# A hybrid decoder trunk on one core: the matrix engine's order written by hand, with a clock that counts product steps

## The chip, the core and the metric

The kernel runs on one core of a Trainium2 chip. A core has a matrix engine (TensorE; PE in the profile, and PEld for its weight loads), a vector engine (VectorE, DVE), a scalar engine (ScalarE, ACT), GpSimd (POOL), and SyncE (SP), whose queue issues every DMA of this kernel. Each engine works off its own queue in the order in which the program put it there. Engines wait for each other through semaphores. The metric is the device time of one execution in microseconds (us).

## What is computed

One decoder layer for 2,048 tokens of width 1,024, in float32. Three groups of heads share one input projection and one output projection. Two of the three kinds (HGRN2, here "h", and GLA, here "g") are gated linear recurrences; retention ("r") is one with a fixed decay. Cut to what matters:

```python
h = rms_norm(x) * (1.0 + sc1) + sh1
proj = h @ w_in[l]                               # 1024 -> all heads' q, k, v, gates
o_r = retention_chunkwise(rotary(rq), rotary(rk) * 64**-0.5, rv, log_gamma)
o_h = gated_state_chunkwise(silu(hq), key_h, hi, log_f)      # S_t = diag(f_t) S_{t-1} + k_t^T v_t
o_a = gated_state_chunkwise(aq, ak * 32**-0.5, av, g_log)    # o_t = q_t S_t
o = concat([rms_norm(o_r)*silu(rg), rms_norm(o_h)*silu(hg), rms_norm(o_a)*silu(ag)]) * head_gain
x = x + g1 * (o @ w_out)
h = rms_norm(x) * (1.0 + sc2) + sh2
u = conv3(h @ w_up) + conv_b                     # causal, depthwise
x = x + g2 * ((silu(gate(u)) * val(u)) @ w_down)
out = rms_norm(x) * final_gain
```

The six vectors sh1 to g2 come from `c` through the matrix w_ada (48 rows of 128 outputs).

## The kernel before

**Products.** Float32 accuracy comes from splitting each operand in a rounded high part (hi) and the rest (lo), and from three fast matmuls hi·hi, hi·lo, lo·hi (`split3`, L180 to L182). So each weight piece (128x1024, 512 KB) is loaded, cast to hi on ACT, and subtracted to lo on DVE (`piece`, L166 and L167; `tf512`, L224 and L225; with a gain for the output projection, L172 and L175). The 38 pieces of a block (30 of w_in, 8 of w_out) are prepared anew for each of the four blocks.

**Mixer.** The 2,048 tokens are four blocks of 512. In each block seven units run in the order h0, g, h1, h2, h3, r0, r1. A unit projects (`cf_gemm`, `tf_gemm`, `tf512`), and then has a chain: seven levels for h and g (`gated`), each of which multiplies q by k on PE in float32 (`lv`, L397), copies the result under a mask into `at` on DVE (L406, ACT for the last two), and multiplies q and k by decays on DVE (L411, L413), on which the next level's matmuls wait; then a transpose of k (`kT`), the state update (`u`), the output (`o`), a norm (`post`), and a transpose (`oT`) for the output projection `out_half`, whose results are called y. An r unit has a rotation on DVE (L573 to L579), transposes (`qT`, `kT`), scores (`scr`, L600), `u`, `o`, `post`. The chain of a unit is written behind the projections of the next unit (`flush`), in a block of priority `CHAIN`; Tile's scheduler decides how the two mix on each engine. The second norm (`ss`, `bc`) writes h2 and x1 to DRAM.

**Conditioning.** The 16 rows of w_ada that the first norm needs are reduced at the start (`ada`: 12 on DVE at L148, 4 on POOL and ACT), the other 32 rows in four groups of eight behind the first four units of block 0.

**Channel mixer.** After `mix.close()` new pools are opened. Stage `up` runs twice (s = 0 for tokens of blocks 0 and 1, s = 1 for 2 and 3), 22 columns f each, with 7 products of 12 matmuls for each f (X, Y, Z in PSUM; Strassen-like sums, so 28 operands B are made from h2 before, and 7 operands A for each f); a convolution on DVE and ACT follows, and `gd` goes to DRAM. Stage `down` then runs over four blocks in two halves of 11 steps (d in PSUM), reads `gd` back (`gr`, cast to G), and ends each block with the third norm and the output.

The order of all engines is the scheduler's, by priorities. SP's queue is one list too: a load that stands behind a store waits until the store can go.

Of the kernel before, what the change touches and what calls it, by code (L numbers as in the profile page):

```python
# [16 lines left out]
P = 128  # L17
# [27 lines left out]
POOL_K = (0, 2, 4, 6)  # L45
# [3 lines left out]
CHAIN = 3000  # L49
FIRST = [("hfh0_0", 1), ("hqh0_0", 0), ("vgh0_0_0", 2)]  # L50


@with_exitstack
def trunk(ctx, tc, xT, vecs, cvec, cst, rope, msk, wada, win, walow, wgla, wout, wup, wdown, out):
# [3 lines left out]
    mix = ctx.enter_context(ExitStack())  # L58
    sb = lambda n, b: mix.enter_context(tc.tile_pool(name=n, bufs=b))
    ph = sb("h", 1)  # L60
    pu = sb("unit", 2)
    p1 = sb("const1", 1)
# [4 lines left out]
    pp = mix.enter_context(tc.tile_pool(name="ps", bufs=1, space=PSUM))  # L67
# [7 lines left out]


    def early_ps(name):
        return pp.tile([P, 512], F32, tag="acc", name=name, bufs=4)
# [79 lines left out]
    def piece(src, name, gain=None, ahead=50):  # L158

        with tc.high_priority(offset=ahead):  # L160
            raw = pw.tile([P, 1024], F32, tag="wraw", name="r" + name, bufs=NRAW)
            nc.sync.dma_start(raw[:], src)
            hi = pw.tile([P, 1024], F32R, tag="whi", name="h" + name)
            lo = pw.tile([P, 1024], F32R, tag="wlo", name="l" + name)
            if gain is None:
                S.copy(hi[:], raw[:])  # L166
                V.tensor_tensor(lo[:], raw[:], hi[:], op=ALU.subtract)  # L167
            else:
# [4 lines left out]
                for i, g in enumerate(gain):  # L173
                    sl = slice(i * n, (i + 1) * n)
                    V.scalar_tensor_tensor(lo[:, sl], raw[:, sl], g, hi[:, sl], op0=ALU.mult, op1=ALU.subtract)  # L175
        return hi, lo
# [13 lines left out]
    def cf_gemm(name, src, parts=(slice(0, TB),)):  # L190
        hi, lo = ready.pop(name, None) or piece(src, name)
        ps = acc_ps("ps" + name)
        for ts in parts:
            for k in range(KD):
                sl = slice(k * P, (k + 1) * P)
                split3(ps[:, ts], (hi[:, sl], lo[:, sl]), (h[k][:, 0, ts], h[k][:, 1, ts]), k == 0, k == KD - 1)
        return ps

    def tf_gemm(name, i):
        pss = [acc_ps(f"ps{name}_{j}") for j in range(NCH // 2)]  # L200
        for half in range(2):
            hi, lo = ready.pop(f"{name}_{half}", None) or piece(win[i + half], f"{name}_{half}")
            for c in range(NCH):
                o = pss[c // 2][:, (c % 2) * 256:(c % 2) * 256 + 256]
                for kk in range(4):
# [4 lines left out]
                           k == 0 and c % 2 == 0, k == KD - 1 and c % 2 == 1)  # L210
        return pss

    def tf512(name, i):

        pss = [acc_ps(f"ps{name}_{c}") for c in range(NCH)]
        for q4 in range(4):
            half, sub = q4 // 2, q4 % 2
            src = win[i + half:i + half + 3:2][:, :, sub * 512:(sub + 1) * 512].rearrange("a p n -> p a n")
            with tc.high_priority(offset=50):
# [5 lines left out]
                V.tensor_tensor(lo[:], raw[:], hi[:], op=ALU.subtract)  # L225
            for c in range(NCH):
                cs = slice(c * P, (c + 1) * P)
                for kk in range(2):
# [3 lines left out]
                           (hi[:, :, sl], lo[:, :, sl]), k == 0, k == KD - 1)  # L232
        return pss


    def rstd_bc(acc, name, bc=None, sl=slice(0, TB)):
        c0, n = sl.start // P, (sl.stop - sl.start) // P
        ps = late_ps("ss" + name)
        for c in range(n):
            T.matmul(ps[:, c:c + 1], acc[:, (c0 + c) * P:(c0 + c + 1) * P], ones, start=True, stop=True)  # L240
        return rstd_from(ps, name, bc, sl)

    def rstd_from(ps, name, bc=None, sl=slice(0, TB)):

        n = (sl.stop - sl.start) // P
        x = small("ms" + name, n)
        V.tensor_scalar(x[:], ps[:, 0:n], 1.0 / D, EPS, op0=ALU.mult, op1=ALU.add)
        r = small("rs" + name, n)
        newton(x, r, n)
        ps = late_ps("bc" + name)  # L250
        for c in range(n):
            T.matmul(ps[:, c * P:(c + 1) * P], r[:, c:c + 1].to_broadcast([P, P]), ident, start=True, stop=True)
        if bc is None:
            bc = px.tile([P, TB], F32, tag="bc2", name="rb" + name, bufs=1)
# [751 lines left out]
```

## Time and profile before

| | |
|---|---|
| three runs, median (lowest to highest) | 2848.06 us (2847.24 to 2851.18) |
| the profiled execution's own time | 2853.58 us |
| its span, first to last instruction | 2851.8 us |
| mean granted TensorE clock | 0.962 of full |
| PE busy | 2641.6 us, 93% of the span |
| DVE busy | 2072.0 us, 73% |
| ACT busy | 1141.9 us, 40% |
| DMA moved | 316.94 MB, 111 GB/s over the span |

Durations come from the one profiled execution. "Granted clock" is the share of full speed at which PE was allowed to run in a stretch. A float32 matmul of 128 columns appears as two records, so that "x8" in a row of the timeline stands for four matmuls of the program. In the chain of waits each line is a start, a duration and who held the chain then.

### The profile page before, as it was taken

To read this page: it belongs to the slowest core of one execution; us is meant where nothing else is said; L and a number is where in the kernel's file an instruction comes from. 1 tells how busy PE (TensorE), PEld (TensorE's weight loads), DVE (VectorE), ACT (ScalarE), POOL (GpSimd) and SP (SyncE) were. 2 spreads that over 40 slices of the span, in tenths; PEclk is the share of its full clock that TensorE was granted. 3 is DMA by queue.
4 is the path that set the end of the run, shared out by engine and by line. 5 is a ranking of instruction groups with operands and counts; after the bars stand their busy time and mean duration, and the time that the engine had idled before them with its cause. 6 is when DMAs were issued, how large, how long until landed. Compare 5 with 4: busy or idle time off the path is not lost.

```text
span 2851.8 us, 35540 instructions
## 1 busy us (share of the span) xinstructions
PE 2641.6 (93%) x13396; PEld 2217.7 (78%) x13396; DVE 2072.0 (73%) x3561; ACT 1141.9 (40%) x1869; POOL 116.4 (4%) x189
## 2 busy tenths in 40 slices
PE   5899889998999979998869999989999979999997
PEld 4788777887778868887748888868888868888886
DVE  8887677876778677784678888898888875534442
ACT  4322434334343434332355445555544544332321
POOL 3000000000000000000000000000000000000000
PEclk9989999999999989999979999989999989999998
DMA  6343314131231413212142222232222236645441
GB/s 255 131 138 116 120 59 151 47 130 64 90 111 59 135 49 136 72 60 74 51 171 89 79 79 86 89 133 89 89 83 81 82 132 223 212 148 189 144 141 59
DMA packets 119419, 316.94 MB, mean 111 GB/s; under 512 B 12592, under 2 KB 14160, under 8 KB 119248
## 3 DMA queue, kind: packets, MB, share of 16 engines
q1 hardware_dynamic: 119248, 314.68, 31.4%
q8 instruction: 105, 1.72, 0.2%
q14 instruction: 66, 0.54, 0.1%
HBM read 266.39 MB, written 48.23 MB: 110 GB/s over the span
## 4 chain that ended last, share of the span: by engine, by line
PE 81%; DVE 13%; issue 2%; ACT 2%; DMA 1%; SPq 0%; DVEq 0%; ACTq 0%
PE X L180 6%; PE d L180 6%; PE d L182 6%; PE d L181 6%; PE X L181 6%; PE X L182 6%; PE lvh L397 4%; PE Z L180 3%; PE Z L181 3%; PE Z L182 3%; PE y L180 2%; PE y L181 2%; PE y L182 2%; PE psqkvgr L180 2%; PE psqkvgr L181 2%
## 5 line engine op out<-in xcount | busy, mean ns | idle before, releaser
L180 PE MATMUL X<-B,A 128*128 128x512 f32 x704 | 280.0, 398 | 22.1 <-ACT B L711 16.1
L180 PE MATMUL d<-G,hd 128*128 128x512 f32 x704 | 275.5, 391 | 15.3 <-ACT G L711 15.3
L181 PE MATMUL X<-B,A 128*128 128x512 f32 x704 | 279.3, 397 | 1.0 <-DVE B L712 1.0
L182 PE MATMUL X<-B,A 128*128 128x512 f32 x704 | 278.3, 395 | 0.0
L182 PE MATMUL d<-G,ld 128*128 128x512 f32 x704 | 275.5, 391 | 0.0
L181 PE MATMUL d<-G,hd 128*128 128x512 f32 x704 | 275.4, 391 | 0.0
L886 DVE TENSOR_TENSOR ld<-rd,hd 128x1024 fp32r<-128x1024 f32 x88 | 107.7, 1224 | 152.1 <-ACT hd L885 151.8
L397 PE MATMUL lvh<-qbd,kh 128*128 128x128 f32 x896 | 138.5, 302 | 50.8 <-DVE kh L413 25.5
L397 PEld LDWEIGHTS lvh<-qbd,kh 128*128 128x128 f32 x896 | 122.2, 208 | 72.4 <-issue 27.2
L180 PEld LDWEIGHTS X<-B,A 128*128 128x128 f32 x704 | 134.6, 191 | 55.3 <-ACT B L711 17.5
L180 PEld LDWEIGHTS d<-G,hd 128*128 128x128 f32 x704 | 132.9, 189 | 42.9 <-ACT G L711 15.7
L885 ACT CAST hd<-rd 128x1024 fp32r<-128x1024 f32 x88 | 92.3, 1048 | 182.8 <-PE d L181 176.3
L181 PEld LDWEIGHTS X<-B,A 128*128 128x128 f32 x704 | 135.1, 192 | 30.5 <-DVE B L712 2.9
L182 PEld LDWEIGHTS X<-B,A 128*128 128x128 f32 x704 | 134.9, 192 | 28.2
L181 PEld LDWEIGHTS d<-G,hd 128*128 128x128 f32 x704 | 132.7, 189 | 28.0 <-DVE G L712 0.4
L182 PEld LDWEIGHTS d<-G,ld 128*128 128x128 f32 x704 | 132.8, 189 | 27.5
L180 PE MATMUL Z<-B,A 128*128 128x512 f32 x352 | 138.2, 393 | 9.4 <-ACT B L711 9.4
L182 PE MATMUL psvgh<-hvgh,ha 128*128 128x256 f32 x512 | 146.6, 286 | 0.0
L180 PE MATMUL psvgh<-hvgh,ha 128*128 128x256 f32 x512 | 146.3, 286 | 0.0
L181 PE MATMUL psvgh<-lvgh,ha 128*128 128x256 f32 x512 | 146.1, 285 | 0.0
L181 PE MATMUL Z<-B,A 128*128 128x512 f32 x352 | 138.0, 392 | 3.1 <-DVE B L712 3.1
L182 PE MATMUL Z<-B,A 128*128 128x512 f32 x352 | 137.6, 391 | 0.0
(388 smaller groups left out, 6562.4 us busy)
## 6 DMA issues: line engine op xcount, KB each, us to landing
rd<-wdown SPq DMA_DIRECT2D x88, 512.0 KB, 3.5
wada<-wada SPq DMA_DIRECT2D x48, 512.0 KB, 3.7
rv<-wup SPq DMA_DIRECT2D x44, 512.0 KB, 3.5
rg<-wup SPq DMA_DIRECT2D x44, 512.0 KB, 3.4
gd<-yv SPq DMA_DIRECT2D x44, 512.0 KB, 2.6
gr<-gd SPq DMA_DIRECT2D x88, 256.0 KB, 3.6
x<-xT SPq DMA_DIRECT2D x64, 256.0 KB, 4.8
rvgh<-win SPq DMA_DIRECT2D x32, 512.0 KB, 3.5
```

What stands on the lines that cost most here:

```text
L180: T.matmul(ps, lhs[0], rhs[0], start=first, stop=False, skip_group_check=more)
L181: T.matmul(ps, lhs[0], rhs[1], start=False, stop=False, skip_group_check=more)
L182: T.matmul(ps, lhs[1], rhs[0], start=False, stop=last, skip_group_check=more)
L397: T.matmul(ps[:, c * P:(c + 1) * P].rearrange("p (h n s) -> p h n s", h=2, s=s), kq[:, c * P:(c + 1) * P], rhs, start=True, stop=True)
L885: S.copy(hi[:], raw[:])
L886: V.tensor_tensor(lo[:], raw[:], hi[:], op=ALU.subtract)
```

## The change

1. **PE's order is written by hand.** After unit h0 of block 0, `tc.manual_schedule` keeps PE's instructions in the order of the code. A `Clock` counts: after each product step `adv` adds that step's time (0.227 us a matmul of 512 columns, 0.12 of 256, 0.224 in float32). A chain is now a generator that yields the gap to its next step; when the clock has passed it, the step's matmuls are let in between the projections that are being written. One chain is in its line at a time; the last step (`oT`) follows 12 us later beside the next chain. All other engines are still scheduled; DVE work of a chain has a higher priority.
2. **Weights are kept.** In block 0 each lo part of w_in, and both gained parts of w_out, are stored to DRAM (`keep`); blocks 1 to 3 load them instead of computing them (ACT still casts hi for w_in).
3. **Conditioning rows are spread**: one of the other 32 rows at each weight piece.
4. **Decays ahead**: the products of decays (`decays`) are computed before the chain; in a level the products of q and k come before the masked copy.
5. **One set of pools.** The up and down stages take over the mixer's buffers, ring by ring, and the same PSUM tags; the order is up 0, down 0 and 1, up 1, down 2 and 3. Norms 1, 2 and 3 are cut in two steps (`rstd`) that the clock places between later products. The first norm of block 0 sums its squares on PE.

The core of the diff:

```diff
+M512, M256, MF = 0.227, 0.12, 0.224
+LEVEL_GAP = (3.2, 4.8)
+POST_GAP = 12.0
+class Clock:
+    def at(self, us, fn):
+        heapq.heappush(self.due, (self.t + us, self.n, fn))
+        self.n += 1
+    def _next(self):
+        t, _, fn = heapq.heappop(self.due)
+        self.t = max(self.t, t)
+        fn()
+    def adv(self, us):
+        self.t += us
+        while self.due and self.due[0][0] <= self.t:
+            self._next()
+    def until(self, done):
+        while not done():
+            self._next()
...
+    def keep(key, t):
+        kept[key] = pdr.tile([P, 1024], F32, tag=f"kept{key}", name=f"kept{key}")
+        nc.sync.dma_start(kept[key][:], t.bitcast(F32))
...
-    def piece(src, name, gain=None, ahead=50):
+    def piece(src, name, key, gain=None, ahead=50):
+        if later:
+            ada(later.pop(0), False, True)
...
+            if key + "h" in kept:
+                nc.sync.dma_start(hi[:].bitcast(F32), kept[key + "h"][:])
+                nc.sync.dma_start(lo[:].bitcast(F32), kept[key + "l"][:])
+                return hi, lo
...
             if gain is None:
                 S.copy(hi[:], raw[:])
-                V.tensor_tensor(lo[:], raw[:], hi[:], op=ALU.subtract)
+                if key + "l" in kept:
+                    nc.sync.dma_start(lo[:].bitcast(F32), kept[key + "l"][:])
+                else:
+                    V.tensor_tensor(lo[:], raw[:], hi[:], op=ALU.subtract)
+                    keep(key + "l", lo[:])
...
                 split3(ps[:, ts], (hi[:, sl], lo[:, sl]), (h[k][:, 0, ts], h[k][:, 1, ts]), k == 0, k == KD - 1)
+                adv(3 * M512)
...
         for li, s in enumerate(LEVELS):
...
+            with tc.high_priority(offset=CHAIN):
+                ev = tree[li]
...
+            adv(4 * len(subs) * MF)
+            yield LEVEL_GAP[two]
...
+        yield None
+        for i, o in enumerate(os):
+            yield POST_GAP if i == 0 else 3.0
+            transposed(b, pos + i, o, f"{name}_{i}")
+            adv(4 * MF)
...
+        clock.chain(gated(nm, b, u, pos, kq, decay, subs, qk, selh), 6.0)
+        tok_evac(subs[0][2:], tf_gemm("vg" + nm, 4 * u + 2))
...
+            if b == 0 and i == 0:
+                ctx.enter_context(tc.manual_schedule(engines={mybir.EngineType.PE}))
+                later += range(16, 48)
+            if i == 0 and b:
+                clock.until(lambda: None not in oTs[b - 1])
+                out_finish(b - 1)
+        if b + 1 < NB:
+            norm1_h(b + 1)
+        else:
+            B = low_inputs(0, tmp)
+        clock.until(lambda: None not in oTs[b][:4])
+        out_half(b, 0)
+    clock.until(lambda: None not in oTs[NB - 1])
+    mix.close()
...
+    B, rest = up_inputs(0, B)
+    out_finish(NB - 1, lambda: first.append(up_weights(0, 0)))
+    rest[0]()
+    up_stage(0, first[0], B)
+    clock.until(lambda: ("n2", NB - 1) in done)
+    down_block(0)
+    A, B = down_block(1, lambda: (up_weights(1, 0), up_inputs(1, low_inputs(1, t2k))[0]))
+    up_stage(1, A, B)
+    down_block(2)
+    down_block(3)
```

Three places in the queues show what moves. Names carry block, unit and level: `lvh2_3_8` is level 8 of unit h3 in block 2, `psqkvgr2_1_0` the projection of r1 in block 2, `y3_1_0` the first product of the output projection's second half in block 3.

PE, block 2, where h3's chain meets the r units; before:

```order
L182 MATMUL psqkvgr2_0_3_8183<-hqkvgr2_0_3_8276,ha2_7_5900 128x512
L397 MATMUL lvh2_3_4_8365<-qbd1_108,kh2_3_7776 128x128 x4
L397 MATMUL lvh2_3_8_8374<-qbd1_108,kh2_3_7776 128x128 x4
L584 MATMUL qTr2_0_8330<-c_all_86,rar2_0_8318 128x128 x4
L586 MATMUL kTr2_0_8331<-c_all_86,kkr2_0_8178 128x128 x4
L180 MATMUL psqkvgr2_1_0_8481<-hqkvgr2_1_0_8487,ha2_0_5851 128x512
```

and of the change:

```order
L528 MATMUL lvh2_3_4_8395<-qbh2_3_7778,kh2_3_7661 128x128 x4
L250 MATMUL psqkvgr2_1_0_8258<-hqkvgr2_1_2_8405,ha2_4_5724 128x512
L251 MATMUL psqkvgr2_1_0_8258<-lqkvgr2_1_2_8406,ha2_4_5724 128x512
L252 MATMUL psqkvgr2_1_0_8258<-hqkvgr2_1_2_8405,ha2_4_5724 128x512
L250 MATMUL psqkvgr2_1_0_8258<-hqkvgr2_1_2_8405,ha2_5_5731 128x512
L251 MATMUL psqkvgr2_1_0_8258<-lqkvgr2_1_2_8406,ha2_5_5731 128x512
L252 MATMUL psqkvgr2_1_0_8258<-hqkvgr2_1_2_8405,ha2_5_5731 128x512
L250 MATMUL psqkvgr2_1_1_8259<-hqkvgr2_1_2_8405,ha2_4_5724 128x512
L251 MATMUL psqkvgr2_1_1_8259<-lqkvgr2_1_2_8406,ha2_4_5724 128x512
L252 MATMUL psqkvgr2_1_1_8259<-hqkvgr2_1_2_8405,ha2_4_5724 128x512
L465 MATMUL oTh2_2_0_8418<-c_all_86,oh2_2_0_8299 128x128 x4
```

Before, levels 4 and 8 stand side by side between two projections; in the change nine matmuls of r1's projection and the transpose of h2's output follow level 4, and three more matmuls before level 8 comes; r0's transposes come some 110 rows later, in the output projection.

PE, block 3, around the last transpose `oTr3_1`; before:

```order
L182 MATMUL y3_1_3_11630<-oTr3_0_11491,lwo3_1_1_11604 128x512
L354 MATMUL oTr3_1_11548<-c_all_86,or3_1_11527 128x128 x4
L180 MATMUL y3_1_0_11569<-oTr3_1_11553,hwo3_1_0_11559 128x512
L180 MATMUL y3_1_1_11584<-oTr3_1_11553,hwo3_1_0_11559 128x512
L180 MATMUL y3_1_2_11613<-oTr3_1_11553,hwo3_1_1_11603 128x512
```

and of the change:

```order
L484 MATMUL or3_1_11651<-vr3_1_11022,atr3_1_11641 128x64 x2
L465 MATMUL oTr3_0_11685<-c_all_86,or3_0_11565 128x128 x4
L465 MATMUL oTr3_1_11693<-c_all_86,or3_1_11664 128x128 x4
L250 MATMUL y3_1_0_11813<-oTh3_2_0_11187,hwo3_1_0_11809 128x512
L251 MATMUL y3_1_0_11813<-oTh3_2_0_11187,hwo3_1_0_11809 128x512
```

Before, 36 matmuls of the output projection's second half stand ahead of `oTr3_1`; in the change none does.

SP, at the border from up to down; before (gd1_21 is the last store of stage up):

```order
L814 DMA gd1_21_235<-yv1_21_18575 128x1024
L880 DMA gr0_0_18600<-gd0_0_192 128x512
L880 DMA gr0_1_18605<-gd0_1_193 128x512
L880 DMA gr0_2_18640<-gd0_2_194 128x512
L880 DMA gr0_3_18645<-gd0_3_195 128x512
```

and of the change, at the border from up 1 to down 2:

```order
L915 DMA rd2_0_4_20553<-wdown 128x1024
L1053 DMA gr2_10_20583<-gd1_10_218 128x512
L1053 DMA gr2_11_20589<-gd1_11_219 128x512
L1053 DMA gr2_12_20625<-gd1_12_220 128x512
L1053 DMA gr2_13_20630<-gd1_13_221 128x512
...
L1070 DMA y1_2_4_21179<-x1d2_4_142 128x512
L1070 DMA y1_2_4_21179<-x1d2_5_143 128x512
L1006 DMA gd1_21_229<-yv1_21_20364 128x1024
L1053 DMA gr2_14_20665<-gd1_14_222 128x512
```

Before, every load of `gr` stands behind the last store; in the change the loads up to `gr2_13` stand ahead of it.

More of the change, by code (lines that the diff above doesn't have):

```diff
@@ L1 @@
+import heapq
 import math
@@ L608, in chain @@
+        ps = late_ps("u" + nm)
+        for c in range(NCH):
+            T.matmul(ps[:, c * P:(c + 1) * P], kk[:, c, :], v[:, c, :], start=True, stop=True)
+        with tc.high_priority(offset=CHAIN):
             for c in range(NCH):
@@ new lines, in out_finish, with take, hc_tile @@
+        clock.at(4.0, rstd(acc, f"n2_{b}", bc[:], then))
+    nth = {"hc": 0, "w4": 0}
+    def take(ring, places):
+        nth[ring] += 1
+        return places[(nth[ring] - 1) % len(places)]
+    def hc_tile(name):
+        pool, tag, bufs, whole = take("hc", HC)
+        if whole:
+            t = (pool or pg).tile([P, 2, 512], F32R, tag=tag, name=name, bufs=bufs)
+            return t[:, 0, :], t[:, 1, :]
+        hi, lo = (pool.tile([P, 512], F32R, tag=tag, name=n + name, bufs=bufs) for n in "hl")
+        return hi[:], lo[:]
```

885 lines of the change are left out of this document (485 added, 400 removed).

## The prediction

> **What bounds the kernel now.** I read the totals first, then busy time by stage, then the chain of waits at the borders of stages.
>
> ```profile
> span 2851.8 us, 35540 instructions
> PE 2641.6 (93%) x13396; PEld 2217.7 (78%) x13396; DVE 2072.0 (73%) x3561; ACT 1141.9 (40%) x1869; POOL 116.4 (4%) x189
> 0.00:62.00 62.00, 28.56 (x157) 24.80 (x158) 51.74 (x89) 31.05 (x47) 22.99 (x25) 1.00 0.73 269
> 62.00:384.00 322.00, 283.19 (x1582) 243.05 (x1581) 250.75 (x522) 108.27 (x202) 2.94 (x4) 0.89 0.35 122
> 384.00:722.00 338.00, 316.57 (x1884) 272.10 (x1884) 254.72 (x549) 129.88 (x244) 7.74 (x10) 0.97 0.27 92
> 722.00:1060.00 338.00, 316.59 (x1887) 272.35 (x1886) 254.79 (x549) 130.10 (x243) 7.74 (x10) 0.97 0.27 92
> 1060.00:1394.00 334.00, 314.05 (x1869) 270.59 (x1868) 236.31 (x510) 117.27 (x227) 6.71 (x8) 0.98 0.22 78
> 1394.00:1480.00 86.00, 56.75 (x227) 43.80 (x225) 62.95 (x121) 35.42 (x62) 0.23 (x3) 0.78 0.44 153
> 1480.00:1885.00 405.00, 402.87 (x1765) 332.54 (x1764) 342.87 (x428) 202.35 (x300) 30.69 (x85) 0.99 0.23 84
> 1885.00:1930.00 45.00, 33.08 (x110) 22.67 (x109) 41.57 (x63) 24.14 (x41) 3.06 (x3) 0.81 0.47 163
> 1930.00:2328.00 398.00, 397.32 (x1754) 328.79 (x1753) 338.91 (x419) 202.41 (x297) 34.26 (x41) 1.00 0.24 88
> 2328.00:2350.00 22.00, 6.74 (x18) 4.72 (x17) 13.17 (x14) 7.41 (x10) 0.00 (x0) 0.61 0.49 159
> 2350.00:2829.00 479.00, 478.84 (x2134) 396.42 (x2133) 212.15 (x276) 150.59 (x198) 0.00 (x0) 1.00 0.47 163
> 2829.00:2852.00 23.00, 7.00 (x30) 5.82 (x28) 12.10 (x26) 2.97 (x5) 0.00 (x0) 0.61 0.24 91
> 1550.00:1600.00 50.00, 50.00 (x222) 41.43 (x221) 43.29 (x54) 23.45 (x36) 3.60 (x11) 1.00 0.20 74
> ```
>
> The columns of a stretch are its length, the busy time of PE, PEld, DVE, ACT, POOL, the granted clock, the DMA share and GB/s. PE is the bound, but busy time hides low clock, so I count what PE has to do. A full stretch (the last row) gives 50/222 = 0.225 us for a matmul of 512 columns. Two more prices:
>
> ```profile
> 1370.44 0.89 PE ur L607 x8
> 52.18 0.12 PE psvgh L180
> ```
>
> Four float32 matmuls take 0.89, so 0.222 each; one of 256 columns 0.12. One mixer block has 16 x 24 x 0.225 (output) + 10 x 24 x 0.225 and 3 x 96 x 0.225 and 4 x 96 x 0.12 (projections) + 4.6 (alow, z) + 381 float32 matmuls x 0.222 + 8 (scores, small ones) = 305 us, the output projection being 16 x 12, so 43 us of it. Up is 2 x 22 x 84 x 0.225 = 831, down 4 x 528 x 0.225 = 475. With block 0's small extras all PE work is 2528 us: **324 us of the span are lost** to idle PE or low clock. Points in the chain of waits say where:
>
> ```profile
> 383.55 1.30 PE scr L600 x6
> 721.84 1.30 PE scr L600 x6
> 1060.05 1.30 PE scr L600 x6
> 1393.80 1.73 PE scr L600 x8
> 1449.20 1.22 PE X L180 x2
> 2328.35 0.24 PE Z L182
> 2338.55 4.59 DMA gr<-gd
> 2343.84 0.79 PE d L180
> 2829.17 0.24 PE d L182
> ```
>
> The first four are r1's scores in blocks 0 to 3. Work up to the first is 276, between them 304.5, 304.6 and 302.5, to X 28.6, from X to the last Z 831.2, then 479.5 to the last d. Losses: **start and block 0, 107.5; blocks 1 to 3, 33.8 + 33.6 + 31.2 = 98.6; end of mixer 26.8; X to Z 48.2; Z to the last d 21.3; tail 22.4.** The 48.2 is nearly all at two borders: 1885 to 1930 does 110 x 0.225 = 24.8 of work in 45 (20), the rest (27) lies before 1480. The stretches between are full.
>
> **The change part by part.** PE keeps its work: the same matmuls, plus 28 of one column in the start. So the question is the losses.
>
> *Levels.* A level needs its matmuls, then L411 and L413, then the next matmuls; L406 follows now.
>
> ```profile
> 234.45 2.06 PE lvh L397 x8
> 238.31 2.06 PE lvh L397 x8
> 242.18 2.04 PE lvh L397 x8
> 69.18 1.14 PE lvh L397 x8
> 72.11 1.14 PE lvh L397 x8
> L406 DVE COPY_PREDICATED ath<-m_all,lvh 128x512 f32<-128x512 uint32 x80 | 75.7, 946 | 37.1 <-PE lvh L397 36.1
> L411 DVE TENSOR_TENSOR qbd<-qbd,eh 128x512 f32<-128x512 f32 x96 | 66.0, 688 | 20.9 <-PE lvh L397 20.7
> L413 DVE TENSOR_TENSOR kh<-kh,eh 128x256 f32<-128x256 f32 x96 | 40.2, 419 | 0.0
> L397 PE MATMUL lvh<-qbd,kh 128*128 128x128 f32 x896 | 138.5, 302 | 50.8 <-DVE kh L413 25.5
> ```
>
> Bare, a level takes 72.11 - 69.18 = 2.93; with a w_ada row between, 3.86, and both held L406 in the path. Written by hand, the next level stands after 3.2 + 0.9, rounded up to a product step: about 4.3. Without L406 the need is 1.14 + 0.69 + 0.42 + 0.1 = 2.35. So 1.9 us are left for one foreign DVE instruction, and PE works meanwhile. A g level has 7.2 against 2.0 + 2 x 0.69 + 0.42. PE can wait little here.
>
> *Kept weights.* Blocks 1 to 3 lose 30 subtractions of 1.225 and 32 of about 0.48 each on DVE, against loads:
>
> ```profile
> L225 DVE TENSOR_TENSOR lqkvgr<-rqkvgr,hqkvgr 128x1024 fp32r<-128x1024 f32 x32 | 39.2, 1225 | 52.8 <-ACT hqkvgr L224 52.8
> rvgh<-win SPq DMA_DIRECT2D x32, 512.0 KB, 3.5
> ```
>
> That is 37 + 15 = 52 of the 255 us of DVE in a block; 203 for 305 of PE remain. It adds 38 loads of 0.5 MB, 19 MB to some 31 MB (92 GB/s x 338 us): 50 MB in 310 us is 161 GB/s, under the 269 that the start moved. In the order a raw load stands some four pieces ahead of its use, about 33 us, against 3.5 to land. I cost it at nothing; the cover is that lead, and if it went, each of 38 pieces would cost up to 3.5 + 1.
>
> *Blocks 1 to 3.* Most of their 33.8 lies at the r units, where projections ran out beside the chain (the first pair of rows in the change). In the change h3's and r0's chains lie between products throughout. Full stretches still lose where DVE is late: PE's waits ahead of `lvh` are 50.8 us over four blocks (row L397), 13 a block, on a busier DVE. Bounds: 4 (a third of that) and 20 (no better than half of the present gap closed). I take 10, near the 13: **98.6 to 30, so -69.**
>
> *Block 0.* Here DVE does everything as before: 51.7 + 250.8 = 302 us up to 384, less seven additions of 0.69 in the first norm. It idled 82. The rows of w_ada, now one at each piece, fill gaps that had no DVE work. Against it: SP has three stores of lo parts ahead of the last three rows of w_ada, up to 7 us later at the start (three loads of 0.5 MB at 269 GB/s, 1.9 each, and 1.2 for lo), and each raw load stands behind the store of the piece before, a loop of 3.5 + 1.05 (cast) + 1.225 + 1 to 4 of DVE queue, 7 to 10 us for a piece that PE uses for 8. Bounds for this stretch: 335 (DVE idle 40) and 375 (nearly unchanged). I take 355: **-28**.
>
> *End of the mixer.*
>
> ```profile
> 1402.88 0.70 DVE or L626
> 1408.83 0.64 PE oTr L354 x4
> L712 DVE TENSOR_TENSOR B<-hr_0b,B 128x512 fp32r<-128x512 f32 x6 | 4.0, 688 | 0.0
> ```
>
> `oTr3_1` now stands ahead of all of the second output half, so PE waits for r1's norm with nothing beside it: 1408.83 - 1402.88 = 6.0 and the 0.4 before, after 1.6 for the masked scores; 2.5 for matmuls at half clock behind such a pause (row 1394:1480 has clock 0.78). In return X starts without h2's way through DRAM, norm 2 runs beside it, and B's first eight operands exist. But product 6 of f = 0 needs B6 of k = 3: between the last y on DVE and that stand 45 instructions, 32 of about 0.69 and 13 of 0.17, so 22 to 24 us, and PE has three products of 2.7 for it. That costs 14, and 2 for clock. Sum 26.5 against 26.8 + 27 = 54: **-27** (-15 to -38).
>
> *Borders.* At 1885 the operands B for s = 1 were the wait; they are now made during down 1, as G's places come free two a step (5.4 us). At 2328 PE waited for `gr`, which stood behind the last store on SP; now fourteen loads of `gr` stand ahead. The 20 + 17 (22 less 18 x 0.225, less 1 of warm work) become about 3, one each for three borders: **-34** (-24 to -37). *Tail:* outputs are made in place, so two waits for an output's buffer go: **-2**.
>
> Sum: 69 + 28 + 27 + 34 + 2 = 160. Span 2691.8; with 1.8 around it (2853.6 was the execution's own time) 2693.6. The median of the runs is 5.5 under the profiled execution, so **2688 us**.
>
> [...] PE waited 50.8 us ahead of `lvh`, with projections behind in its queue. [...]
>
> **The rivals.**
> - *Fuller than I think* (0.2): 4 lost in each block (DVE has 100 us to spare in 305), block 0 in 340, the border of the mixer at its better bound: 18 + 15 + 9 less, 2646. For it: full stretches of stage up lose nothing. Against: stalls of 13 a block on `lvh` today.
> - *Order only half fits* (0.2): 20 lost in each block, block 0 in 375, the mixer's end 38: 30 + 20 + 12 more, 2750. For it: DVE's order holds places with seven to nine foreign instructions between two levels (norm of g, squares of norm 1), 6 us where 4.3 are planned.
> - *Kept loads late, or the queue full* (0.06): the change takes DVE's work away but each piece waits 1 us for its lo: 3 x 38 = 114 more, about 2800. Against: the lead of four pieces.
> - *Slower* (0.04): steps let in too early, everywhere. A block has 35 levels and some 25 other steps, 240 in all. To eat the 160 each must stop PE by 0.67; so from a mean of 4.3 + 0.67 = 5.0 us for an h level on it decides, against 2.35 bare and 3.86 at the worst above. At 5.3 it would be 240 x 1.0 - 160 = 80 slower, 2930. The bare levels speak against it.
>
> **How the numbers follow.** My forecast has 0.5, with its own range 2655 to 2725. Leaving out the last two rivals and the outer edge of the first two, the range is 2640 to 2755. What this measurement can tell from no change is 0.2%, 5.7 us. Faster: 0.5 + 0.2 + 0.2 + 0.06, less 0.01 for a sum that just cancels = 0.95; same 0.01; slower 0.04.
>
> **What would show it.** r1's scores about 315 apart in blocks 1 to 3, and the first near 355; DVE near 203 busy in such a block; PE idle 6 ahead of `oTr` and about 14 ahead of product 6 once, in block 3's end; no pause over 2 us at the three borders; d and X stretches full as now. Wrong: idle PE ahead of `lv` by over 1 us a level (hand order too tight), ahead of projections on `lo` DMAs (loads late), or up's stretches under 99% busy (fewer buffers in the rings, which I cost at nothing because A's ring of eight places, not the raw weights, paces them).

## The result, and the profile after

The changed kernel takes **2708.21 us** (median of four runs, 2702.77 to 2711.09) against 2849.62 (2847.24 to 2852.82) before: 0.9501 of it, with an interval of 0.9482 to 0.952. The forecast was 2688, with a range of 2640 to 2755. The profiled execution took 2702.77 us, its span 2700.9 against 2691.8 forecast: 9 over. The rest of the 20 by which the median missed is the choice of execution: the profiled one of before stood 5.5 over its median, which the forecast took off; this one stands 5.4 under it.

The head of the page of the changed kernel, and its busy time by stage (columns as in the prediction):

```profile
span 2700.9 us, 35764 instructions
PE 2594.2 (96%) x13452; PEld 2200.2 (81%) x13452; DVE 1904.4 (71%) x3408; ACT 1100.5 (41%) x1805; POOL 152.3 (6%) x250
```

```profile
0.00:68.00 68.00, 37.44 (x169) 32.34 (x170) 40.19 (x69) 29.36 (x44) 20.92 (x27) 0.97 0.68 246
68.00:384.00 316.00, 277.25 (x1653) 240.91 (x1652) 251.60 (x553) 108.54 (x213) 13.65 (x24) 0.95 0.53 183
384.00:684.00 300.00, 299.17 (x1855) 265.15 (x1855) 208.01 (x504) 123.93 (x236) 13.26 (x22) 1.00 0.53 182
684.00:987.00 303.00, 302.43 (x1886) 268.79 (x1886) 205.71 (x496) 116.82 (x220) 15.81 (x26) 1.00 0.50 168
987.00:1288.00 301.00, 301.00 (x1874) 267.63 (x1873) 195.47 (x462) 104.26 (x200) 12.79 (x20) 1.00 0.46 158
1288.00:1324.00 36.00, 29.15 (x138) 24.47 (x137) 28.81 (x54) 12.37 (x22) 0.21 (x3) 0.91 0.56 190
1324.00:1360.00 36.00, 22.11 (x92) 16.88 (x91) 32.73 (x62) 20.93 (x36) 0.58 (x1) 0.76 0.45 152
1770.00:2012.00 242.00, 242.00 (x1070) 199.45 (x1070) 136.02 (x178) 90.41 (x125) 5.09 (x3) 1.00 0.53 182
2440.00:2686.00 246.00, 243.96 (x1072) 199.65 (x1070) 106.84 (x132) 74.18 (x94) 0.00 (x0) 1.00 0.43 147
```

The order of stages is now up 0 (from 1323), down 0 and 1 (1770 to 2012), up 1, down 2 and 3 (2440 to 2686). Blocks 1 to 3 are full at clock 1.00: PE is busy 299 of 300 us and so on, and DVE fell to 208, 206 and 195 us a block, near the 203 of the forecast. What is left is at the start, in block 0, and between 1288 and 1360.

The timeline of the changed kernel has r1's scores, the marks of the prediction, at:

```profile
372.07 1.89 PE L758 MATMUL scr<-qbr,kcr 128*128 128x256 f32 x8
683.60 1.89 PE L758 MATMUL scr<-qbr,kcr 128*128 128x256 f32 x8
986.92 1.89 PE L758 MATMUL scr<-qbr,kcr 128*128 128x256 f32 x8
1287.55 1.89 PE L758 MATMUL scr<-qbr,kcr 128*128 128x256 f32 x8
```

By the prices of the prediction the work between them, in the order of the changed program, is 311.1, 304.6 and 303.1; they stand 311.5, 303.3 and 300.6 apart. So nothing is lost there (the prices are rounded, hence a little less than nothing), where 99 were lost before. The waits of PE from 384 to 1288 (who waited for whom: us in total, times, longest) are two lines:

```profile
PE lvh L528 <- DVE kh L538: 1.1, 2, 0.6
PE pshqh L250 <- ACT hhqh L230: 0.3, 1, 0.3
```

Before, the longest two of the same three blocks (384 to 1394) were

```profile
PE lvh L397 <- DVE ath L406: 17.2, 7, 5.1
PE lvh L397 <- DVE kh L413: 10.0, 9, 2.2
```

so 27.2 us ahead of `lvh` (the 50.8 of the prediction's row are for all four blocks). In the changed kernel no line names a load of a kept part.

The end of the mixer and the start of up, in the timeline and in three stretches:

```profile
1299.61 1.09 PE L465 MATMUL oTr<-c_all,or 128*128 128x128 f32 x4 [5.75 <-DVE or L459]
1337.47 0.79 PE L250 MATMUL X<-B,A 128*128 128x512 f32 x1 [6.15 <-ACT B L851]
1339.07 0.80 PE L251 MATMUL X<-B,A 128*128 128x512 f32 x1 [0.80 <-DVE B L852]
1347.22 0.80 PE L250 MATMUL X<-hB,A 128*128 128x512 f32 x1 [6.94 <-ACT hB L851]
...
1294.00:1296.00 2.00, 0.00 (x0) 0.00 (x0) 1.59 (x4) 1.02 (x2) 0.00 (x0) 1.00 1.03 273
1296.00:1303.00 7.00, 3.39 (x11) 2.89 (x12) 4.35 (x15) 0.91 (x2) 0.00 (x0) 0.51 0.29 109
1299.60:1302.90 3.30, 3.29 (x10) 2.82 (x11) 1.29 (x2) 0.81 (x2) 0.00 (x0) 0.50 0.00 0
```

PE is idle 5.75 ahead of `oTr3_1` (forecast 6) and 6.15 + 0.80 + 6.94 = 13.9 ahead of product 6 (forecast 14). The clock is at half for about 7 us, but it falls some 2 us into the first pause (from 1293.9 to 1299.6), so that only 3.3 us of work behind it run at half clock; half of that, 1.6 us, is the estimate of what it costs.

### The profile page after: what moved, and what is told of

The parts are those of the page before. It is cut to its first block, busy times and chain, and to the rows that moved or that the text cites. A ratio compares the mean times of both kernels' runs of the same rounds, so it can differ in the third digit from the quotient of the medians.

```text
span 2700.9 us, 35764 instructions
## 1 busy us (share of the span) xinstructions
PE 2594.2 (96%) x13452; PEld 2200.2 (81%) x13452; DVE 1904.4 (71%) x3408; ACT 1100.5 (41%) x1805; POOL 152.3 (6%) x250
## 4 chain that ended last, share of the span: by engine, by line
PE 89%; DVE 6%; DMA 2%; ACT 1%; issue 1%; POOL 0%; SPq 0%; DVEq 0%; ACTq 0%
PE X L250 6%; PE X L251 6%; PE X L252 6%; PE d L252 6%; PE d L251 6%; PE d L250 6%; PE lvh L528 3%; PE Z L252 3%; PE Z L251 3%; PE Z L250 3%; PE y L252 2%; PE y L250 2%; PE psqkvgr L251 2%; PE psqkvgr L252 2%; PE y L251 2%; PE psqkvgr L250 2%
## 5 line engine op out<-in xcount | busy, mean ns | idle before, releaser
L252 PE MATMUL d<-G,ld 128*128 128x512 f32 x608 | 238.5, 392 | 0.0
L251 PE MATMUL d<-G,hd 128*128 128x512 f32 x608 | 237.6, 391 | 0.0
L250 PE MATMUL d<-G,hd 128*128 128x512 f32 x608 | 237.5, 391 | 0.0
L250 PE MATMUL X<-B,A 128*128 128x512 f32 x572 | 225.1, 394 | 6.8 <-ACT B L851 6.1
L251 PE MATMUL X<-B,A 128*128 128x512 f32 x572 | 225.4, 394 | 0.8 <-DVE B L852 0.8
L252 PE MATMUL X<-B,A 128*128 128x512 f32 x572 | 224.6, 393 | 0.0
L852 DVE TENSOR_TENSOR A<-s,A 128x512 fp32r<-128x512 f32 x176 | 120.8, 687 | 66.4 <-ACT A L851 66.4
L251 PEld LDWEIGHTS d<-G,hd 128*128 128x128 f32 x608 | 114.1, 188 | 25.5
L250 PEld LDWEIGHTS d<-G,hd 128*128 128x128 f32 x608 | 114.1, 188 | 25.0
L252 PEld LDWEIGHTS d<-G,ld 128*128 128x128 f32 x608 | 114.1, 188 | 24.4
L250 PEld LDWEIGHTS X<-B,A 128*128 128x128 f32 x572 | 107.6, 188 | 32.3 <-ACT B L851 6.6
L251 PEld LDWEIGHTS X<-B,A 128*128 128x128 f32 x572 | 107.4, 188 | 24.7 <-DVE B L852 1.3
L252 PEld LDWEIGHTS X<-B,A 128*128 128x128 f32 x572 | 107.6, 188 | 24.2
L528 PEld LDWEIGHTS lvh<-qbh,kh 128*128 128x128 f32 x896 | 116.6, 193 | 9.2 <-issue 2.9
L528 PE MATMUL lvh<-qbh,kh 128*128 128x128 f32 x896 | 121.6, 279 | 1.6 <-DVE kh L538 1.6
L252 PE MATMUL Z<-B,A 128*128 128x512 f32 x308 | 121.0, 393 | 0.0
L251 PE MATMUL Z<-B,A 128*128 128x512 f32 x308 | 120.8, 392 | 0.0
```

The lines of the kernel that those rows point to most:

```text
L250: T.matmul(ps, lhs[0], rhs[0], start=first, stop=False, skip_group_check=more)
L251: T.matmul(ps, lhs[0], rhs[1], start=False, stop=False, skip_group_check=more)
L252: T.matmul(ps, lhs[1], rhs[0], start=False, stop=last, skip_group_check=more)
L528: T.matmul(ps[:, c * P:(c + 1) * P].rearrange("p (h n s) -> p h n s", h=2, s=s), kq[:, c * P:(c + 1) * P], rhs, start=True, stop=True)
L852: V.tensor_tensor(lo, src, hi, op=ALU.subtract)
```

## The experiments

Each loss below is the time between two marks less the work between them, at the prices of the prediction and in the order of that kernel's own program. The marks are g's first chain step of block 1 (g1), r1's first scores of block 3 (r1), the first product of up (X) and the last product of down (d). g1 is taken in place of block 0's scores, as in some orders waits that belong to block 0 fall behind these. Times are medians; the runs without an interval are single. Four executions of the changed kernel lie 8 us apart, so a difference of less than that from a single run tells nothing; the losses are read within one execution.

| kernel | us | start to g1 | g1 to r1 | r1 to X | X to d |
|---|---|---|---|---|---|
| before | 2849.62 | 116 | 90 | 26 | 72 |
| changed | 2708.21 | 101 | -5 | 8 | 48 |
| e1_aligned | 2703.34 | 104 | -5 | 8 | 45 |
| e2_nokeep | 2695.72 | 71 | 17 | 9 | 49 |
| e3_sched | 2698.76 | 98 | -4 | 1 | 54 |
| e4_ring | 2684.74 | 76 | -4 | 9 | 53 |
| e5_sched_nokeep | 2680.21 | 76 | 4 | 0 | 50 |
| e6_blocks | 2734.74 | 93 | 44 | 0 | 48 |
| e7_half_early | 2813.69 | 101 | 101 | 10 | 50 |
| e12_half_mid | 2767.94 | 93 | 62 | 10 | 53 |
| e9_before_late_half | 2852.19 | 117 | 94 | 22 | 72 |
| e8_layout | 2696.70 | 102 | -4 | 9 | 39 |
| e10_all | 2663.06 | 65 | 4 | 0 | 37 |
| e11_start | 2663.72 | 65 | 6 | 0 | 40 |

### What filled blocks 1 to 3

**Without the kept parts** (e2_nokeep):

```diff
     def keep(key, t):
-        kept[key] = pdr.tile([P, 1024], F32, tag=f"kept{key}", name=f"kept{key}")
-        nc.sync.dma_start(kept[key][:], t.bitcast(F32))
+        return
```

> Nothing is stored to DRAM and loaded back: every block makes its lo parts (and both parts of the output projection) anew, as before the change; the order by hand stays. Theory (the order alone brings most of the gain in blocks 1 to 3): DVE is busy about 255 of 305 us in a block and PE loses 4 to 10 us in each, so r1's scores in blocks 1 to 3 stand 309 to 315 us apart (303 with the kept parts). Rival (the kept parts bring it): over 325 apart, 20 or more lost in each block. For block 0, where the changed kernel has r1's first scores at 372: if the stores of the kept parts hold the raw loads up in SP's queue, as the prediction feared, they come at 355 to 360 without them; if the ring of two raw places, which the rows of w_ada share, or DVE paces block 0, they stay at 368 to 375.

r1's scores stand 322.7, 313.8 and 301.7 apart; 17 are lost behind g1 in all three, nearer to the theory's 4 to 10 a block than to the rival's 20, although DVE is as busy again as before the change (profile by stage, block 1):

```profile
341.00:663.00 322.00, 311.45 (x1912) 275.08 (x1911) 258.25 (x572) 132.32 (x253) 15.82 (x26) 0.98 0.31 104
```

The expectation's 309 to 315 holds for the second gap alone; the first is longer, and the third shorter. The kept parts are worth 21 us in blocks 1 to 3. But block 0's scores come at 340.60 in place of 372.07, earlier than either case allowed: storing them costs 30 there. The net is a loss.

**Without the fixed order** (e3_sched):

```diff
             if b == 0 and i == 0:
-                ctx.enter_context(tc.manual_schedule(engines={mybir.EngineType.PE}))
                 later += range(16, 48)
```

> The one line that keeps PE's instructions in the order of the code is taken out: Tile's scheduler orders PE too, by the priorities; everything else of the change stays, the kept parts too. Theory (the order is what brings the gain): with DVE at 205 of 305 us in a block PE still waits for levels that stand side by side, and blocks 1 to 3 lose 10 to 30 us each: r1's scores 315 to 335 apart. Rival (a freer DVE is enough): 303 to 307 apart, as with the order by hand.

r1's scores stand 343.6, 303.4 and 300.6 apart, with work of 320.5, 304.6 and 303.1 between them. The 23 lost in the first are block 0's: the scheduler took the scores at 337.39 ahead of products whose weights came late, and the waits follow behind the mark (PE from 337 to 470):

```profile
PE y L252 <- DVE lwo L243: 7.0, 1, 7.0
PE y L250 <- ACT hwo L240: 5.5, 3, 2.9
PE pshfh L250 <- ACT hhfh L230: 3.5, 1, 3.5
```

Behind g1 nothing is lost (-4), and r1 to X falls from 8 to 1, as the scheduler puts products ahead of `oTr3_1`. The theory fell: the line that fixes the order is not what brought the gain.

**Without either** (e5_sched_nokeep, both edits):

> Neither the fixed order on PE nor the kept parts: the scheduler orders PE by the priorities of the new code, and every block makes its lo parts anew. Without either one alone, PE lost 19 us in blocks 1 to 3 (time between r1's scores of block 0 and of block 3, less the work that stands between them at the full rate); with both 3 less than nothing, before the change 99. Theory (each covers for the other, and one of them brought the 100): 60 to 100 lost. Rival (the losses add, and what brought most of it is still in this kernel: where the clock puts the steps in the code, or the output projection's new place): 30 to 50 lost.

4 lost behind g1. By the expectation's own measure, from scores to scores, it is 26, of which 20 lie between the first two scores, where the longest wait (PE from 318 to 449) is again one for block 0's late weights:

```profile
PE y L251 <- DVE lwo L242: 6.9, 1, 6.9
```

Neither case holds by either measure: both parts away, the blocks behind g1 are nearly as full as with both, and the kernel is faster than the change, 2680.21 us. What fills the blocks must be in what is left of the change, above all where the code puts things.

**Chains in one piece** (e6_blocks: scheduler, kept parts, and)

```diff
-LEVEL_GAP = (3.2, 4.8)
-POST_GAP = 12.0
+LEVEL_GAP = (0.0, 0.0)
+POST_GAP = 0.0
...
-        clock.chain(gated(nm, b, u, pos, kq, decay, subs, qk, selh), 6.0)
+        clock.chain(gated(nm, b, u, pos, kq, decay, subs, qk, selh), 14.0)
```

> PE is ordered by the scheduler, and all gaps of the clock are 0: the chain of a unit is written in one piece, level behind level, behind its own values (start 14 in place of 6 for h, 24 in place of 14 for g), as it was before the change; kept parts, decays ahead and the place of the output projection stay. Theory (the spread of the steps is what counts): the levels stand side by side again and blocks 1 to 3 lose 50 to 100. Rival (the scheduler fills between levels by itself, and a freer DVE or the output projection's place brought the gain): 15 to 30, as with the scheduler and the gaps.

44 lost between g1 and r1 (64 from scores to scores, as the theory had it). The same stretch of the two kernels, the changed one first:

```profile
400.00:1200.00 800.00, 798.86 (x5022) 711.53 (x5022) 539.09 (x1283) 308.34 (x571) 40.43 (x65) 1.00 0.50 170
```

```profile
400.00:1200.00 800.00, 784.14 (x4724) 668.45 (x4723) 532.69 (x1244) 293.31 (x543) 39.66 (x64) 1.00 0.48 160
```

PE is nearly as busy (784 of 800), but got 298 matmul records less done, 6%; at the prices of the prediction the work in the stretch falls by about as much. Busy time hides short stops, most of them ahead of levels; the count does not. The spread of the steps in the code is worth about half of the 95.

**The output projection's first half early.** I had not named its move in the prediction: before, it was written behind h1's chain, now at the block's end. e7_half_early puts it behind h2's projections, e12_half_mid behind h3's (the same edit with `i == 4`):

```diff
             if i == 0 and b:
                 clock.until(lambda: None not in oTs[b - 1])
                 out_finish(b - 1)
+            if i == 3:
+                clock.until(lambda: None not in oTs[b][:4])
+                out_half(b, 0)
...
-        clock.until(lambda: None not in oTs[b][:4])
-        out_half(b, 0)
```

> The first half of the output projection is written behind h2's projections, near its old place, in place of the block's end; order by hand, clock and kept parts stay. Theory (the half at the block's end is what h3's and r0's and r1's chains lie beside): without it they run into the next block's first projections, norm 1 and the second half wait for them, and blocks 1 to 3 lose 20 to 40. Rival (the clock finds products wherever they stand): under 6 lost. In block 3, which has no next block, r0's and r1's chains then have nothing beside them: X starts 20 to 35 us later behind r1's scores there by either theory.

> The changed kernel with the first half of the output projection behind h3's projections, where h1's output has long been transposed, so that no step has to be forced ahead as it was behind h2. Theory (what stands at the block's end counts): blocks 1 to 3 still lose 30 to 60, ahead of the next block's first projections, as norm 1 of the next block and r1's chain have no products beside them. Rival (the early half lost by the forced steps alone): under 12 lost in blocks 1 to 3, only block 3's end pays.

101 and 62 lost: in e7_half_early far more than the 20 to 40 expected, in e12_half_mid just over the 30 to 60. What both theories of e7_half_early expected of block 3's end did not come: X starts 36.6 us behind r1's scores there, against 35.9 in the changed kernel. PE's waits over blocks 1 to 3, e7_half_early and then e12_half_mid:

```profile
PE lvh L528 <- DVE kh L538: 20.0, 15, 1.8
PE pshfh L250 <- ACT ha L356: 18.9, 2, 9.6
PE oTh L465 <- DVE oh L459: 9.9, 3, 3.3
```

```profile
PE pshfh L250 <- ACT ha L356: 19.7, 2, 10.0
PE oTh L465 <- DVE oh L459: 10.5, 3, 3.6
```

`pshfh <- ha` is the next block's first projection, which waits for norm 1 with no product in between, as the theory had it. The waits for `kh` and `oh` are steps that `until` forced ahead (it runs the steps that are due next at once, until the transposes are written); behind h3 most for `kh` are gone, those for `oh` not. So part of the 62 is still the forcing, and it is an upper bound for the place.

**The same move in the old kernel** (e9_before_late_half):

```diff
-        if i == 2:
-            out_half(b, 0, oTs[b][:4])
...
         if b + 1 < NB:
             norm1_h(b + 1)
+        out_half(b, 0, oTs[b][:4])
     flush()
```

> The kernel before, with one edit: the first half of the output projection is written at the block's end, behind norm 1 of the next block, in place of behind h1's chain. No clock, no kept parts, no order by hand. Written early in the changed kernel it cost 113 us. Theory (its place is what the blocks gained by): PE loses 30 to 60 us less than before up to the first product of up (233 before), and the time falls to 2790 to 2820. Rival (the old code, with a chain in one piece at high priority, can't use it, and the early place cost so much only because the clock was forced forward there): within 15 us of 2850, on either side.

2852.19 against 2851.27, ratio 1.0003 (0.9993 to 1.0012): nothing. PE's waits in blocks 1 to 3 there:

```profile
PE qTr L584 <- DVE rar L577: 19.1, 3, 6.4
PE lvh L397 <- DVE ath L406: 17.1, 6, 5.1
```

The masked copies still hold the levels up, and r1's transposes now wait for its rotation. So the place alone gives nothing, the spread without it loses up to 62 (e12_half_mid) or 101, the place without the spread 44: full blocks need both, and neither the fixed order nor the kept parts. Part 4 of the change (decays ahead, the masked copy behind the products) and the higher priority of the chains' DVE work stand in every one of these kernels but the old one and were not taken out by themselves, so their share in the step from 90 to 44 is not known.

### Block 0

e4_ring loads the later rows of w_ada into another ring:

```diff
-            raw = pw.tile([P, D], F32, tag="wraw", name=f"wada{m}", bufs=NRAW)
+            raw = (px.tile([P, D], F32, tag="xy", name=f"wada{m}", bufs=4) if m < 40 else
+                   pw.tile([P, D], F32, tag="wraw", name=f"wada{m}", bufs=NRAW))
```

> In block 0 the later rows of w_ada (16 to 39) are loaded into the ring of x, which is idle between the first norm and the output projection, so that both raw places serve the weight pieces; only rows 40 to 47 still share them. Theory (in block 0 the ring of raw places is the loop: load 3.5 to 5, cast 1.05, DVE's queue and 1.23, and only then the next load, as every second place goes to a row of w_ada): r1's first scores come at 352 to 362 in place of 372, and the time falls by 10 to 20 us. Rival (DVE, busy 252 of 316 us there, or the stores in SP's queue pace it): 368 to 375, no change beyond 4 us.

345.68, and 2684.74 us: the theory holds, by more than it said. In the changed kernel DVE, SP and PE read there:

```profile
356.26 0.47 DVE L243 SCALAR_TENSOR_TENSOR lwo<-rwo,vec,hwo 128x256 fp32r<-128x256 f32 x1
...
356.76 0.33 SPq L212 DMA_DIRECT2D kepto1l<-lwo  x1
357.14 0.42 SPq L228 DMA_DIRECT2D rwo<-wout  x1
...
355.19 0.80 PE L252 MATMUL y<-oTg,lwo 128*128 128x512 f32 x1 [7.12 <-DVE lwo L243]
```

The next raw load (of `rwo`) leaves only when the last lo of the piece before is made: raw weights have two places, and the load needs that piece's, as the other has gone to a row of w_ada; it also stands behind that piece's store. Taking away the stores (e2_nokeep) won 30 up to g1, the other ring 25; together, with the scheduler's order (e10_all), 36. That either one opens most of the loop is shown; why one is enough is not. So the stores cost 30 only while the places are shared: e4_ring, which keeps them, stands 5 behind e2_nokeep at g1.

### The rate of the products in up and down

In the changed kernel a step of up takes 19.37 us (19.31 in up 1) in place of 19.04. Grouped by the place of the moving operand (its byte address in SBUF, which the program fixes and the profile doesn't show), from the starts of neighbouring matmuls, three matmuls of one k take 0.680 us in some places and up to 0.706 in others. Eight of the 28 places stand behind the halo (the two columns of each tile that up keeps for its second pass). e1_aligned pads the halo, e8_layout moves these places further:

```diff
-    halo = pg.tile([P, 2 * NF, 2], F32, tag="halo", name="halo")
+    halo = pg.tile([P, 96], F32, tag="halo", name="halo")[:, 0:4 * NF].rearrange("p (t n) -> p t n", n=2)
```

> The halo tile is 352 bytes a partition and stands ahead of half of the operand places of the channel mixer, so these begin at 32 bytes past a multiple of 64; here it is padded to 384 bytes, and nothing else changes. In the changed kernel a matmul of 512 columns whose moving operand lies so takes 0.2344 us in up and 0.2335 in down, the others 0.2286 and 0.2270; before, with all of them on multiples of 64, 0.2268. Theory (the place in SBUF sets the rate): all come back to 0.2268, up loses 0.0035 x 3696 = 13 us and down 0.0020 x 2112 = 4, so 17 us less: about 2691 us against 2708, a step of up 19.05 us apart again in place of 19.36. Rival (other engines or DMAs that run beside up slow the matmuls, as the order up, down, up, down brings new neighbours): the step stays at 19.36 and the time within 3 us of 2708.

2703.34 us, ratio to before 0.9487 (0.9471 to 0.9504), which overlaps with the change's. The step is 19.26: the padding brought a third of what it should, so it is the place, but not the multiple of 64.

```diff
-    halo = pg.tile([P, 2 * NF, 2], F32, tag="halo", name="halo")
+    def halo(t):
+        if not halos:
+            halos.append(pg.tile([P, 2 * NF, 2], F32, tag="halo", name="halo"))
+        return halos[0][:, t, :]
...
+    first_t2m = t2m("first")
+    G.memset(first_t2m[:, 0:1], 0.0)
```

> Padding the halo to a multiple of 64 bytes did not bring the full rate back: three matmuls of one k take 0.680 us where the moving operand's place is 2688 bytes past a multiple of 4096 (all places of before, and those of h and a4k now), and 0.696 to 0.705 in the places of the new pool (992, then 1024 past it), whatever DVE, ACT and DMA do beside them. Here the halo is allocated last and a tile of 2 KB first, so that these eight places too lie 2688 past a multiple of 4096. Theory (the place relative to 4096 sets the rate): they take 0.680, a step of up 19.1 us in place of 19.36, and 11 to 14 us less in all, 2694 to 2697 against 2708. Rival (places above 160 KB are slow as such): they stay at 0.696, as with 1024, and the time stays within 4 us of the padded one (2703).

2696.70 us, ratio 0.9459 (0.944 to 0.9478), below the change's whole interval. A full stretch of 370 us of up 1, first of the changed kernel, then of e8_layout:

```profile
2060.00:2430.00 370.00, 370.00 (x1612) 302.39 (x1611) 305.36 (x386) 185.31 (x275) 36.92 (x39) 1.00 0.25 88
```

```profile
2060.00:2430.00 370.00, 369.32 (x1631) 305.48 (x1629) 310.04 (x391) 187.49 (x279) 38.42 (x39) 1.00 0.25 90
```

1612 matmuls became 1631; the steps are 19.04 again in up 1, as the theory had it. The first matmul of one k of product 2 and that of the next, in the changed kernel (992 past a multiple of 4096) 0.70 us apart, in e8_layout (2688 past it) 0.68:

```profile
2209.99 0.40 PE L250 MATMUL Y<-B,A 128*128 128x512 f32 x1
...
2210.69 0.40 PE L250 MATMUL Y<-B,A 128*128 128x512 f32 x1
```

```profile
2208.82 0.39 PE L250 MATMUL Y<-B,A 128*128 128x512 f32 x1
...
2209.50 0.39 PE L250 MATMUL Y<-B,A 128*128 128x512 f32 x1
```

In up 0 nothing came back (1776 matmuls from 1360 to 1770, against 1775): PE now met eight waits for `u`, 4.1 us in sum. So of the 17 estimated for the places, 9 came back.

### Together

e10_all: e5_sched_nokeep, e4_ring and e8_layout in one.

> The scheduler orders PE, no part is kept (2680 us together), the later rows of w_ada go through the ring of x, and the operand places lie 2688 past a multiple of 4096. Theory (the layout's gain adds in full, 9 to 12, and the ring's in block 0, where PE still lost 55, in part): 2655 to 2667. Rival (without stores the raw ring is no loop any more, as the run without them had r1's first scores 31 us earlier by itself): the layout alone, 2668 to 2672.

2663.06 us, ratio 0.9346 (0.9328 to 0.9363): 45 us faster than the change. This is inside the theory's range. X to d fell by 13 against e5_sched_nokeep, start to g1 by 10 to 11.

e11_start, on top of it:

```diff
-                with tc.high_priority(offset=150):
+                with tc.high_priority(offset=150 if s or f > 1 else 0):
                     A = up_weights(s, f)
...
-            with tc.high_priority(offset=HOT):
+            with tc.high_priority(offset=HOT if b < NB - 1 else 0):
                 for m in range(KD):
```

> As the run with everything together, and in the start of up two things on DVE stand behind the operands B: the eight products of block 3's norm 2 (5.4 us in one piece at 1306.99 there; its results are read only in the second up) lose their high priority, and the operands A of f = 1 theirs. Theory (what keeps product 6 of f = 0 waiting is DVE's queue, as the prediction counted it): 42 us of almost unbroken DVE work ahead of the last B shrink by 8 to 10, PE's waits in the first 45 us behind X (16 us of idle there) fall by 6 to 10, and the time from 2663 to 2653 to 2658. Rival (the loads set it: four raw places, each reloaded only when the four of the k before are used up): the waits move to the loads of hr, and under 3 us are won.

2663.72 us, ratio 0.9346 (0.9333 to 0.9359): nothing won. The stretch of e10_all, then of e11_start:

```profile
1290.00:1325.00 35.00, 24.03 (x81) 17.01 (x80) 33.42 (x64) 20.03 (x35) 0.00 (x0) 0.76 0.56 187
```

```profile
1290.00:1325.00 35.00, 22.27 (x70) 14.08 (x69) 33.09 (x64) 20.29 (x35) 0.00 (x0) 0.72 0.52 170
```

DVE is busy 33 of 35 us in both. The last operands came 5 us earlier, but PE's 12.6 us of waits (1288 to 1340) only broke up into more and shorter ones (12.7), and the clock stayed low among them (0.72 in the row). The theory's gain did not come. The time is the rival's, but its reason isn't seen either: from 1288 to 1330 DVE and ACT wait only 1.8 us for loads of `hr`. What would shorten this start was not found.

## Why the prediction was right, and where it was not

The time lay 20 us over the forecast and inside its own range of 2655 to 2725. That is luck in part: blocks 1 to 3 gave 33 more than forecast, the start with block 0 and the borders 21 and 20 less, and the errors nearly cancel. Term by term, on the profiled executions:

| term | forecast | measured |
|---|---|---|
| blocks 1 to 3 | -69 | -102 (99 to -3, r1 to r1) |
| start and block 0 | -28 | -7 (107 to 100, up to r1's first scores) |
| end of mixer with the start of up | -27 | -28 (53.5 to 25) |
| borders and the rest from X to d | -34 | -14 (45 to 31) |
| tail | -2 | -3 |

The sum is -154; with 4 us more of work, of the small matmuls of norm 1, the span fell by 151. (The end of the mixer after: 8 up to X, and 1324:1360 holds 76 products of 0.225 and some 2 of small ones, so 17 more are lost. X to d: 72 less 27 before, 48 less 17 after.)

- **The work of a block**: the 16 x 24 in the prediction's sum is a slip; with the 16 x 12 that the same sentence gives it comes to the 305 used.
- **Blocks 1 to 3**: the direction held, the size was low, and the reason was mostly another. I read rightly that "projections ran out beside the chain" at the r units, and that steps would lie between products. But I gave the gain to the fixed order and to a freer DVE. The order moves nothing here (e3_sched), the kept parts 21 (e2_nokeep) or, with the scheduler, 8 (e5_sched_nokeep against e3_sched). What carries it is the spread of the steps (e6_blocks) together with the half of the output projection at the block's end (e7_half_early, e12_half_mid), a move that stood in the code and in no term of mine. My bounds, 4 to 20 lost a block, came from waits on `lvh` as a cost that stays; none stayed.
- **Block 0**: the failed step is "The rows of w_ada, now one at each piece, fill gaps that had no DVE work". They took every second raw place, and the loop that the prediction itself priced at 7 to 10 us a piece became the pace. With the ring given back (e4_ring) the scores came at 345.68, 9 ahead of the 355.
- **Kept weights**: "I cost it at nothing; the cover is that lead" held for the loads, as no wait names one. The stores were the cost: 30 in block 0 while the raw places were shared, more than the 8 to 21 that the loads save.
- **End of the mixer**: right in each pause, 5.75 for 6 and 13.9 for 14; the half clock behind the first cost an estimated 1.6, where 2.5 were forecast. That DVE's queue sets the 13.9 was not confirmed: e11_start took work out of it and won nothing.
- **Borders**: the pauses are gone; from 1360 to 2683 PE waits twice, 0.7 each. But "d and X stretches full as now" was wrong in a way that busy time doesn't show: full, yes, but with a step of up 19.37 long in place of 19.04. By estimate some 17 us of the missing gain went there (0.0035 x 3696 + 0.0020 x 2112: what a matmul of up and of down took over 0.2268 on the mean, times their number), through the places of the new pool; 9 were won back by moving them.
- **The rivals**: "fuller" came true in the blocks alone; "order only half fits", "kept loads late" and "slower" did not: PE waited 1.1 us ahead of `lvh` in three blocks. Block 0 alone came near the 375 of "order only half fits" (372), for another reason. What steps let in too early cost, as "slower" had it, is seen where `until` forced them (e7_half_early: PE waited 20.0 us ahead of `lvh`, 15 times).

## What to carry to other kernels

When a large rewrite is fast, take its parts out one by one: here the fixed order was worth nothing and the kept weights, with the raw places shared, less than nothing, and full blocks came of where two things stand in the code, neither of which does it alone. Ask of every piece of work without a deadline (an output projection, a table row) what it could stand beside, and what ring it takes a place in. And count matmuls in a stretch, not busy time: a PE that was 100% busy did 1% fewer than it can (1612 for 1631), and one that was 98% busy 6% fewer.

## What the runs showed of the hardware

- **The place of an operand in SBUF set the rate of float32r matmuls.** With all moving operands 2688 bytes past a multiple of 4096 (halves of 2 KB, so 640 past one of 2048), three matmuls of 512 columns took 0.680 us (before, e8_layout); in places 1024 past it, 0.696 and more (e1_aligned), and 992 past it, 0.700 to 0.706 (the changed kernel), also where DVE was busy 5 of 20 us and DMA moved 79 GB/s (2640 to 2660 there). The tiles of the weights began 2688 past it in all of these. In up of the changed kernel some places that never moved took 0.693 and came back to 0.680 when their neighbours in the order moved (e8_layout), so the exact relation is not settled.
- **Short pauses cost twice here**, by themselves and by the clock. In the changed kernel's pause of 5.75 us the clock fell to half some 2 us in and was back 3.3 us after work returned. With ten waits of 0.4 to 2.2 us in 35 us the mean was 0.72 (e11_start), in stretches of full and of half clock:

```profile
1298.40:1301.80 3.40, 1.23 (x3) 0.48 (x3) 3.40 (x11) 1.24 (x2) 0.00 (x0) 1.00 0.46 133
1301.80:1308.60 6.80, 5.06 (x15) 3.86 (x15) 6.71 (x14) 3.80 (x7) 0.00 (x0) 0.50 0.40 130
1308.60:1312.00 3.40, 1.23 (x3) 0.48 (x3) 3.40 (x6) 1.25 (x3) 0.00 (x0) 1.00 0.82 280
1312.00:1329.00 17.00, 11.27 (x22) 6.75 (x23) 15.79 (x26) 11.70 (x20) 0.00 (x0) 0.50 0.54 185
```

  No pause in that stretch is longer than 2.2 us, and the clock fell twice behind 3.4 us in which PE was still busy for 1.23; it was back behind 6.8 us at half clock, in which PE was busy for 5.06. What sets the fall and the return was not shown.
